# The second expert table's rows of two token tiles, laid a token to a partition and summed on VectorE instead of TensorE

## Chip, cores and metric

One core of one Trainium2 chip. The metric is the device time of one execution in microseconds; the median of three runs counts. PE is TensorE, DVE VectorE, ACT ScalarE, POOL GpSimd and SP SyncE.

## What is computed

One layer of a decoder trunk for a prompt of 1024 tokens (8 tiles of 128) and 32 sample tokens (a ninth, short tile, number 8 or NT). After the mixers each token chooses 128 experts of 16384 (8 heads, 16 each), and a layer called PEER sums them:

```python
def expert_block(args):
    xk, ik, gk = args                     # 128 tokens, their 8 x 16 experts, their weights
    act = gelu(einsum('nd,nhkd->nhk', xk, peer_u[ik]))
    coef = gk * act
    return einsum('nhk,nhkd->nd', coef, peer_v[ik])
...
x = layer_norm(ALPHA * x + g2 * y, ln2_g, ln2_b)
```

`peer_u` and `peer_v` are tables of 16384 rows of 1024 floats (4 KB a row). All is in float32.

## The kernel before

Four tiles (3 to 6, `DENSE`) go through **all** experts as dense products: 128 key rows of 128 experts. For each key row PE multiplies the split x of the four tiles with a block of `peer_u` (`psd`, 24 products of 512 columns, line 1067), ACT and DVE make the coefficients (`act` and `coef`, lines 1157 to 1165), and PE multiplies those with the block of `peer_v` (`po`, line 1174); DVE adds each `po` to the tile's sum (line 1183). Blocks of both tables are split into two halves of 16 bits by ACT and DVE (`us`, `vs`). Four key rows make a **group**: 96 `po` products, and 72 `psd` products of the next group, since every fourth key row has its `psd` made earlier, in a stage before (it is loaded back as `act`). There are 32 groups, 0 to 31. This is called the dense stage here.

The other five tiles (`GATHERED` = 0, 1, 2, 7, NT) fetch the rows that their tokens chose. For `peer_u` (`u_items`), step k fetches the k-th expert of each of 128 tokens, a token to a partition, by an indirect DMA on POOL's queue (512 KB), and DVE multiplies the tile with the tokens' x and adds along the row (line 1297; called U in the prediction). For `peer_v` (`v_items`), a step fetches the 128 experts of **one** token, an expert to a partition; PE multiplies them with a 128x32 matrix `cexp` that holds that token's 128 coefficients in one column (line 1354), so that the sum over partitions falls on that token's row of the PSUM tiles `acc0` and `acc1`. Two steps are issued together as four products (eight instructions in the trace). `cexp` comes from DVE (line 1344), and the coefficients and indices are transposed on PE for it at the end of `u_items`.

Gathered tiles run one behind another; the u steps of the next tile run beside the v steps of the one before. v rows of tiles 2, 7 and NT land in a ring of `NROW2` = 6 buffers of their own (`rows2`), u rows and the v rows of tiles 0 and 1 in one of 6 (`rows`). Tiles 2 and 7's and NT's v steps, and tile 7's and NT's u steps, lie in the dense stage.

The order is set by `run`: each part (here `g_main`, which runs the dense stage, and `g_gather`) yields costs for PE, DVE and DMA in us, and the part that is earliest on that account goes on; the framework's scheduler then orders the instructions by priority and its own timeline. `g_finish` (line 1411) multiplies a tile's sum with g2, adds x, and makes the LayerNorm.

Of the kernel before, what the change touches and what calls it, by code (L numbers as in the profile page):

```python
# [7 lines left out]
F32 = mybir.dt.float32  # L8
# [6 lines left out]
ALU = mybir.AluOpType  # L15
AX = mybir.AxisListType

P = 128
D = 1024
KD = D // P  # L20
NT = 8
# [22 lines left out]
    ("dense", {"g_gather": 0.8}),  # L44
)
NROW = 6
NROW2 = 6
AMPLE = 96
MB = 2.78
GATHERED = (0, 1, 2, 7, NT)  # L50
DENSE = (3, 4, 5, 6)
# [27 lines left out]
def kernel(ctx: ExitStack, tc: tile.TileContext, A, O):  # L79
    nc = tc.nc  # L80
    mm, tr = nc.tensor.matmul, nc.tensor.transpose
    V, S = nc.vector, nc.scalar
# [1191 lines left out]
    def u_items(t):  # L1274

        smp = t == NT
        n = NS if smp else P
        IF, G = (top[t][2][:, e].rearrange("p h j -> p (h j)") for e in range(2))
        x2 = cur["rows"].tile("x2u", [P, D])
        ii = keep("ii", [P, P], I32, bufs=2)  # L1280
        sv = keep("sv", [P, P], bufs=2)
        if smp:
            fr = keep("fr", [P, NS])
            for q in range(4):
                nc.sync.dma_start(x2[32 * q:32 * q + 32, :], x2_d[t, :NS, :])
                nc.sync.dma_start(fr[32 * q:32 * q + 32, :], IF[:NS, 32 * q:32 * q + 32])
            V.tensor_copy(ii[:, :NS], fr)
        else:
            nc.sync.dma_start(x2, x2_d[t])

        def step(k):
            if not smp and k % 16 == 0:
                V.tensor_copy(ii[:, k:k + 16], IF[:, k:k + 16])  # L1293
            s = gather("peer_u", ii[:, k:k + 1])

            def use():
                V.scalar_tensor_tensor(out=s, in0=s, scalar=1.0, in1=x2, op0=ALU.mult, op1=ALU.mult,  # L1297
                                       accum_out=sv[:, k:k + 1])
            return use

        for k in range(NS if smp else P):
            yield lambda k=k: step(k)

        def finish():
            if smp:
                s2 = keep("cT_", [P, P], bufs=2)[:NS]
                for q in range(4):
                    nc.sync.dma_start(s2[:, 32 * q:32 * q + 32], sv[32 * q:32 * q + 32, :NS])
                a = s2
            else:  # L1310
                a = sv
            S.activation(a[:n], a[:n], AF.Gelu)
            V.tensor_mul(a[:n], a[:n], G[:n])
            pt = psum.tile([P, 2, P], F32, name="ptc", tag="g", bufs=1)
            tr(pt[:, 0, :n], a[:n], ident[:n, :n])
            tr(pt[:, 1, :n], IF[:n], ident[:n, :n])
            cT_ = keep("cT_", [P, P], bufs=2)
            iT = keep("iT", [P, P], I32, bufs=2)
            V.tensor_copy(cT_[:, :n], pt[:, 0, :n])
            V.tensor_copy(iT[:, :n], pt[:, 1, :n])  # L1320
            coef[t] = (cT_, iT)
        yield finish

    def v_items(t):


        smp = t == NT
        cT_, iT = coef[t]
        pv = [psum.tile([P, 512], F32, name=f"acc{e}", tag=f"acc{e}", bufs=1) for e in range(2)]
        nj = 8 if smp else 32  # L1330
        hold = {}
        for j in range(nj):
            for q in range(4):

                def step(j=j, q=q):
                    if j % 2 == 0 and q == 0:
                        ce_ = hold["c"] = cur["rows"].tile("cexp", [P, 2, 4, 32], F32, 2)
                        if smp:
                            cv = cT_[:, 4 * j:4 * j + 8].rearrange("p (j q) -> p j q", q=4)
                            dv = delta[:, :, 32 - 4 * j:64 - 4 * j].rearrange("p (j q) c -> p j q c", q=4)  # L1340
                        else:
                            cv = cT_.rearrange("p (q j) -> p j q", q=4)[:, j:j + 2, :]
                            dv = delta[:, 0:2, 32 - j:64 - j].unsqueeze(2).to_broadcast([P, 2, 4, 32])
                        V.tensor_tensor(out=ce_, in0=cv.unsqueeze(3).to_broadcast([P, 2, 4, 32]), in1=dv, op=ALU.mult)
                    tok = 4 * j + q if smp else 32 * q + j
                    hold[q % 2] = gather("peer_v", iT[:, tok:tok + 1], t not in GATHERED[:2]), hold["c"][:, j % 2, q, :]
                    if q % 2 == 0:
                        return lambda: None
                    rows = hold[0], hold[1]

                    def add(b, e):
                        g = 32 * (q - 1 + b ^ 2 * e)
                        s, l = rows[b]
                        return mm(pv[e][g:g + 32, :], lhsT=l, rhs=s[:, e * 512:e * 512 + 512], start=(j == 0),  # L1354
                                  stop=(j == nj - 1), skip_group_check=True)

                    def use():
                        first = add(1, 0)
                        with tc.issue_after(first.ins):
                            add(1, 1)  # L1360
                            add(0, 0)
                            add(0, 1)
                    return use
                yield step

        def finish():
            src = pv
            if smp:
                src = []
                f = cur["rows"].tile("row", (P, D), F32, NROW)  # L1370
                fs = [f[:, 0:512], f[:, 512:1024]]
                for e in range(2):
                    (S.activation(fs[e], pv[e], AF.Copy) if e else V.tensor_copy(fs[e], pv[e]))
                yield 0, 1.2, 0
                for e in range(2):
                    b = bank("pfold")
                    mm(b[:NS], lhsT=fold, rhs=fs[e], start=True, stop=True)
                    src.append(b)
                yield 1.8, 0, 0
            if R:  # L1380
                yield from g_finish(t, NS if smp else P, src)
            else:
                finish_tile(t, NS if smp else P, src)
        yield finish
# [25 lines left out]

    def g_finish(t, n, src):
        x, g2 = ahead.pop(t)
        z = cur["rows"].tile("row", (P, D), F32, NROW)
        if t == NT:
            for e in range(2):
                c = slice(e * 512, e * 512 + 512)
                V.tensor_mul(z[:n, c], src[e][:n], g2[:n, c])
        else:
            sums_to(z, src)
            V.tensor_mul(z, z, g2)  # L1420
        yield 0, 1.2, 0
        V.tensor_add(z[:n], z[:n], x[:n])
        yield 0, 1.2, 0
        ln_rows(z, n, (R["ln2_g"], R["ln2_b"]))
        yield 0, 4.2, 0
        nc.sync.dma_start(O["y_s"] if t == NT else O["y_p"][t * P:(t + 1) * P, :], z[:n])
        yield 0, 1.2, 1.5
# [136 lines left out]
    def g_gather():  # L1564
# [6 lines left out]
        while todo or us or vs or done:  # L1571
# [20 lines left out]
            elif vs:  # L1592
# [13 lines left out]
                iv += 1  # L1606
                if done[0] == GATHERED[1] and iv == AMPLE:
                    ready.add("ample")
                c = 0.43, 0, 1.46
            else:  # L1610
                yield from wait(need or (todo[0], 0))
                continue
# [113 lines left out]
```

## Time and profile before

| | |
|---|---|
| median of 3 runs | 3274.7 us (3269.59 to 3281.56) |
| the profiled execution | 3260.78 us, its span 3259.1 us |
| busy share of the span | PE 84%, DVE 68%, POOL 41%, ACT 29% |
| mean granted clock of PE | 0.904 of 2.4 GHz |
| moved by DMA | 964.85 MB, mean 296 GB/s |

Busy time of an engine is the time in which at least one of its instructions ran. "Idle before, releaser" is the time an engine sat idle ahead of an instruction, and what ended it. The dense stage takes the span from about 1895 us to the end.

### The profile page before, as it was taken

The numbers are of one execution on the slowest core, as the hardware profiler recorded it, in microseconds if no ns is written. First come the engines' busy times: TensorE is split into PE (matmuls) and PEld (weight loads), VectorE is DVE, ScalarE is ACT, GpSimd is POOL, SyncE is SP. The second block draws the span as 40 slices with busy tenths as digits, with TensorE's granted clock in tenths as the row PEclk, the third lists the DMA queues.
The fourth block names the chain that finished last, engine by engine and source line by source line (L and its number), as shares of the span: only waits on it lengthen the run. The fifth ranks groups of instructions, "written<-read, shape, count | busy, mean of one in ns | idle before, by whom it ended". The sixth has DMA issues, their size and how long they took to land.

```text
span 3259.1 us, 44856 instructions
## 1 busy us (share of the span) xinstructions
PE 2740.2 (84%) x16366; PEld 1409.0 (43%) x16366; DVE 2206.8 (68%) x5763; ACT 938.7 (29%) x1618; POOL 1346.1 (41%) x1096
## 2 busy tenths in 40 slices
PE   6888984487976867998764699999999999999996
PEld 2447942344654425664333333343333433334443
DVE  2443998876788557988878547677677754456557
ACT  3323243111111013333446522222222222223331
POOL 0000366535445454544764527556554534440000
PEclk8888997698977878999886799999999999999998
DMA  8654798899998988888899989999999989994442
GB/s 295 232 180 145 281 350 306 291 321 322 334 328 298 328 315 294 290 289 321 285 326 348 351 298 359 360 363 381 372 378 340 384 300 326 352 321 136 141 129 75
DMA packets 370576, 964.85 MB, mean 296 GB/s; under 512 B 36933, under 2 KB 114884, under 8 KB 366252
## 3 DMA queue, kind: packets, MB, share of 16 engines
q0 software_dynamic: 156672, 570.49, 48.2%
q1 hardware_dynamic: 213684, 391.51, 34.7%
q8 instruction: 128, 2.10, 0.3%
q14 instruction: 92, 0.75, 0.1%
HBM read 892.92 MB, written 69.02 MB: 295 GB/s over the span
## 4 chain that ended last, share of the span: by engine, by line
PE 50%; DMA 14%; DVE 10%; issue 4%; POOL 2%; ACT 2%; SPq 0%; POOLq 0%; DVEq 0%; ACTq 0%
PE po L1174 18%; PE psd L1067 15%; PE acc L1354 6%; DMA row<-in_peer_v,iT 5%; DMA row<-in_peer_u,ii 5%; PE pqr L881 3%; DVE row L1297 3%; PE py L809 2%; POOL row L1270 2%; DMA v<-in_peer_v 1%; PE pvp L280 1%; PE pgm L1054 1%; DMA g<-G_d 1%; ACT gs L1057 1%; PE ps L886 0%
## 5 line engine op out<-in xcount | busy, mean ns | idle before, releaser
L1270 POOL DMA_INDIRECT row<-in_peer_u,ii x544 | 688.4, 1265 | 821.0 <-DVE ii L1293 316.9
L1270 POOL DMA_INDIRECT row<-in_peer_v,iT x544 | 655.4, 1205 | 717.7 <-PE acc L1354 460.5
L1297 DVE SCALAR_TENSOR_TENSOR row<-row,x2u 128x1024 f32<-128x1024 f32 x544 | 657.8, 1215 | 175.8 <-DMA row<-in_peer_u,ii 149.5
L1067 PE MATMUL psd<-xd,us 128*128 128x512 f16 x3072 | 722.6, 387 | 27.6 <-ACT us L1084 24.2
L1174 PE MATMUL po<-vs,coef 128*128 128x512 f16 x3072 | 700.8, 380 | 35.8 <-ACT coef L1164 20.3
L1174 PEld LDWEIGHTS <-coef 128*128 128x128 f16 x3072 | 294.0, 98 | 458.5 <-issue 89.5
L1067 PEld LDWEIGHTS <-us 128*128 128x128 f16 x3072 | 297.1, 100 | 450.8 <-issue 84.4
L1354 PE MATMUL acc<-row,cexp 128*32 128x512 f32 x2176 | 334.2, 665 | 139.5 <-DMA row<-in_peer_v,iT 128.2
L881 PE MATMUL pqr<-x2T,wpq 128*128 128x128 f32 (+1 forms) x2304 | 285.8, 285 | 8.3 <-ACT scores L892 7.0
L881 PEld LDWEIGHTS pqr<-x2T,wpq 128*128 128x128 f32 x2304 | 278.5, 201 | 21.9 <-ACT scores L892 7.2
L1159 DVE SCALAR_TENSOR_TENSOR act<-act,scale,g 128x512 f32<-128x512 f32 x128 | 96.1, 751 | 281.2 <-ACT act L1157 268.1
L1157 ACT ACTIVATE act<-psd,scale 128x512 f32<-128x512 f32 x96 | 65.9, 687 | 640.6 <-PE psd L1067 640.5
L1183 DVE SCALAR_TENSOR_TENSOR acc<-po,scale,acc 128x512 f32<-128x512 f32 x248 | 184.1, 746 | 84.0 <-PE po L1174 83.5
L1138 DVE SCALAR_TENSOR_TENSOR vs<-v,vs 128x1024 f16<-128x1024 f32 x128 | 155.9, 1219 | 62.3 <-ACT vs L1137 62.3
L1137 ACT ACTIVATE vs<-v 128x1024 f16<-128x1024 f32 x128 | 133.5, 1051 | 150.4 <-PE po L1174 90.1
L1054 PE MATMUL pgm<-ab 128*128 128x128 f16 x1024 | 97.3, 250 | 80.6 <-DVE ab L1044 42.8
L1354 PEld LDWEIGHTS acc<-row,cexp 128*32 128x32 f32 x2176 | 47.7, 112 | 266.1 <-DMA row<-in_peer_v,iT 166.6
L809 PE MATMUL py<-wo,Y 128*128 128x512 f32 (+1 forms) x288 | 138.9, 631 | 15.5 <-DMA Y<-ycat_d 14.3
L1057 ACT ACTIVATE gs<-pgm 128x256 f32<-128x256 f32 x256 | 124.6, 639 | 58.7 <-PE pgm L1054 45.9
L280 PEld LDWEIGHTS <-w 128*128 128x128 f16 x2160 | 123.0, 100 | 24.0 <-issue 20.8
L1121 DVE SCALAR_TENSOR_TENSOR us<-u,us 128x1024 f16<-128x1024 f32 x96 | 117.3, 1223 | 22.7 <-ACT us L1120 22.7
L1054 PEld LDWEIGHTS <-ab 128*128 128x128 f16 x1024 | 79.2, 113 | 117.9 <-issue 55.2
(343 smaller groups left out, 2857.1 us busy)
## 6 DMA issues: line engine op xcount, KB each, us to landing
v<-in_peer_v SPq DMA_DIRECT2D x128, 512.0 KB
u<-in_peer_uT SPq DMA_DIRECT2D x96, 512.0 KB
wpq<-in_w_pq SPq DMA_DIRECT2D x64, 512.0 KB
G_d<-gs SPq DMA_DIRECT2D x32, 1024.0 KB
g<-G_d SPq DMA_DIRECT2D x32, 1024.0 KB
wada<-in_w_ada SPq DMA_DIRECT2D x48, 512.0 KB
wf<-in_w_in SPq DMA_DIRECT2D x44, 512.0 KB
wo<-in_w_o SPq DMA_DIRECT2D x32, 512.0 KB
```

What stands on the lines that cost most here:

```text
L280: mm(out, lhsT=x if cs is None else y, rhs=y if cs is None else x, start=(i + k == 0), stop=(i == len(ps) - 1 and k == KD - 1))
L809: mm(py[t, e][:ns[t]], lhsT=Y_[t][:, k + j, :ns[t]], rhs=w[:, j, :], start=(k + j == 0), stop=(k + j == KD - 1))
L881: mm(pq[:, i * P:i * P + ns[t]], lhsT=w[:, k, :], rhs=X2[t][:, k, :ns[t]], start=(k == 0), stop=(k == KD - 1))
L1054: mm(pg[:, j, :], lhsT=ab[:, 0, t4 + j, :], rhs=ab[:, 1 + e, t4 + j, :], start=(e == 0), stop=(e == 1))
L1057: S.activation(gs[e][:, :, t0:t0 + 4].rearrange("p c t -> p t c"), pg[:, :, 64 * e:64 * e + 64], AF.Copy)
L1067: mm(ps, lhsT=us[a][:, k, :], rhs=xd[:, :, b, k, :], start=(m == 0), stop=(m == 23))
L1138: V.scalar_tensor_tensor(out=vs[:, 1], in0=v, scalar=SV, in1=vs[:, 0], op0=ALU.mult, op1=ALU.subtract)
L1174: mm(po, lhsT=d[:, a, i * P:(i + 1) * P], rhs=vs[:, b, c % 2, :], start=(m == 0), stop=(m == 3 * GROUP - 1))
L1183: V.scalar_tensor_tensor(out=a, in0=po, scalar=scale[:, 3:4], in1=a, op0=ALU.mult, op1=ALU.add)
L1270: nc.gpsimd.indirect_dma_start(out=s[:], out_offset=None, in_=A[table], in_offset=bass.IndirectOffsetOnAxis(ap=idx, axis=0))
L1297: V.scalar_tensor_tensor(out=s, in0=s, scalar=1.0, in1=x2, op0=ALU.mult, op1=ALU.mult, accum_out=sv[:, k:k + 1])
L1354: return mm(pv[e][g:g + 32, :], lhsT=l, rhs=s[:, e * 512:e * 512 + 512], start=(j == 0), stop=(j == nj - 1), skip_group_check=True)
```

## The change

For tiles 2 and 7 (`BY_TOKEN`), `u_items` ends without the transposes. A v step then fetches the k-th expert of each of 128 tokens, as the u steps do, and DVE multiplies it with that token's k-th coefficient (a column of `sv`) and adds it to a tile `vsum` in SBUF. After 128 steps `g_finish` goes on from `vsum`. The `rows2` ring shrinks by one buffer; a v step of these tiles is booked as 1.22 us of DVE instead of 0.43 us of PE. Tiles 0, 1 and NT stay as they were.

```diff
-NROW2 = 6
+NROW2 = 5
 AMPLE = 96
+BY_TOKEN = (2, 7)
...
             V.tensor_mul(a[:n], a[:n], G[:n])
+            if t in BY_TOKEN:
+                coef[t] = (sv, ii)
+                return
             pt = psum.tile([P, 2, P], F32, name="ptc", tag="g", bufs=1)
...
+    def v_items_by_token(t, cf, ix):
+
+        z = cur["rows2"].tile("vsum", (P, D))
+
+        def step(k):
+            s = gather("peer_v", ix[:, k:k + 1], True)
+
+            def use():
+                if k == 0:
+                    V.tensor_scalar(z, s, cf[:, 0:1], None, op0=ALU.mult)
+                else:
+                    V.scalar_tensor_tensor(out=z, in0=s, scalar=cf[:, k:k + 1], in1=z, op0=ALU.mult, op1=ALU.add)
+            return use
+
+        for k in range(P):
+            yield lambda k=k: step(k)
+
+        def finish():
+            yield from g_finish(t, P, z)
+        yield finish
+
     def v_items(t):
...
         cT_, iT = coef[t]
+        if t in BY_TOKEN:
+            yield from v_items_by_token(t, cT_, iT)
+            return
...
     def g_finish(t, n, src):
         x, g2 = ahead.pop(t)
-        z = cur["rows"].tile("row", (P, D), F32, NROW)
-        if t == NT:
+        z = src if t in BY_TOKEN else cur["rows"].tile("row", (P, D), F32, NROW)
+        if t in BY_TOKEN:
+            V.tensor_mul(z, z, g2)
+        elif t == NT:
...
-                c = 0.43, 0, 1.46
+                c = (0, 1.22, 1.46) if done[0] in BY_TOKEN else (0.43, 0, 1.46)
```

The order of instructions at three places. First DVE in the middle of the dense stage, from the `act` of one key row on. Before, with a `cexp` product now and then (`act`, `coef`, `us`, `vs` and `acc` are the dense stage's; `row,sv` is U):

```order
L1159 SCALAR_TENSOR_TENSOR act<-act,scale,g_18832 128x512
L1121 SCALAR_TENSOR_TENSOR us<-u,us 128x1024
L1138 SCALAR_TENSOR_TENSOR vs<-v,vs 128x1024
L1297 SCALAR_TENSOR_TENSOR row,sv<-row,x2u 128x1024
L1165 TENSOR_TENSOR coef<-act,coef 128x512
L1297 SCALAR_TENSOR_TENSOR row,sv<-row,x2u 128x1024 x2
L1159 SCALAR_TENSOR_TENSOR act<-act,scale,g_18832 128x512
```

and with the change, at a like place:

```order
L1160 SCALAR_TENSOR_TENSOR act<-act,scale,g_18088 128x512
L1122 SCALAR_TENSOR_TENSOR us<-u,us 128x1024
L1298 SCALAR_TENSOR_TENSOR row,sv<-row,x2u 128x1024
L1339 SCALAR_TENSOR_TENSOR vsum<-row,sv,vsum 128x1024
L1298 SCALAR_TENSOR_TENSOR row,sv<-row,x2u 128x1024
L1166 TENSOR_TENSOR coef<-act,coef 128x512
L1139 SCALAR_TENSOR_TENSOR vs<-v,vs 128x1024
L1298 SCALAR_TENSOR_TENSOR row,sv<-row,x2u 128x1024
L1160 SCALAR_TENSOR_TENSOR act<-act,scale,g_18088 128x512
L1339 SCALAR_TENSOR_TENSOR vsum<-row,sv,vsum 128x1024
```

The sums (`vsum`) now stand between the operations that make the coefficients for PE. Second, the same engine where tile 7's sum ends:

```order
L787 SCALAR_TENSOR_TENSOR vsum<-vsum,mv,r_ln_b 128x1024
L1423 SCALAR_TENSOR_TENSOR x1f<-x1f,r_ln_g 32x1024
L1424 SCALAR_TENSOR_TENSOR x1f<-r_ln_b,x1f 32x1024
L1372 TENSOR_TENSOR cexp<-cT__22846,delta 128x256 x2
L1401 COPY row<-acc_23586 128x512
L1447 TENSOR_TENSOR row<-pfold,g2s 32x512 x2
```

The last `cexp` of the sample tile and the copy of its sum stand behind tile 7's LayerNorm (line 787). Third, the end of POOL's queue, before:

```order
L1270 DMA row<-in_peer_u,ii 128x1024 x3
L1270 DMA row<-in_peer_v,iT 128x1024 x2
L1270 DMA row<-in_peer_u,ii 128x1024 x3
L1270 DMA row<-in_peer_v,iT 128x1024 x3
L1270 DMA row<-in_peer_u,ii 128x1024
L1270 DMA row<-in_peer_v,iT 128x1024
L1270 DMA row<-in_peer_u,ii 128x1024 x2
L1270 DMA row<-in_peer_v,iT 128x1024 x128
```

and with the change:

```order
L1271 DMA row<-in_peer_v,ii 128x1024 x16
L1271 DMA row<-in_peer_u,ii 128x1024 x6
L1271 DMA row<-in_peer_v,ii 128x1024
L1271 DMA row<-in_peer_u,ii 128x1024 x26
L1271 DMA row<-in_peer_v,ii 128x1024 x123
L1271 DMA row<-in_peer_v,iT 128x1024 x32
```

Before, the last 128 gathers are the end of tile 7's (96) and the sample tile's 32. With the change nearly all of tile 7's v rows come behind the last u row, and the sample tile's 32 behind those; on PE the sample tile's 64 products stand in one piece, five groups ahead of the end.

## Rows read from the trace of the kernel before

**Rows 1.** The page: busy time of each engine (us, share of the span, instructions), and the shares of the chain of work that ended last, by engine.

```profile
PE 2740.2 (84%) x16366; PEld 1409.0 (43%) x16366; DVE 2206.8 (68%) x5763; ACT 938.7 (29%) x1618; POOL 1346.1 (41%) x1096
...
PE 50%; DMA 14%; DVE 10%; issue 4%; POOL 2%; ACT 2%; SPq 0%; POOLq 0%; DVEq 0%; ACTq 0%
```

**Rows 2.** Windows of 100 us: length, then busy us (instructions) of PE, PE's weight loads, DVE, ACT and POOL, PE's granted clock, DMA share, GB/s.

```profile
400.00:500.00 100.00, 87.53 (x655) 50.41 (x652) 95.36 (x312) 46.02 (x67) 63.13 (x46) 0.96 0.98 347
500.00:600.00 100.00, 43.44 (x250) 29.04 (x250) 89.91 (x230) 26.10 (x45) 69.13 (x54) 0.66 0.86 301
...
800.00:900.00 100.00, 95.67 (x574) 60.64 (x574) 69.16 (x233) 11.28 (x31) 49.53 (x44) 0.88 0.92 334
900.00:1000.00 100.00, 81.26 (x545) 55.87 (x546) 80.83 (x346) 17.14 (x38) 45.97 (x41) 0.81 0.94 339
...
2300.00:2400.00 100.00, 92.71 (x458) 37.12 (x457) 73.72 (x105) 27.68 (x35) 58.35 (x50) 0.98 1.00 377
...
2500.00:2600.00 100.00, 100.00 (x497) 40.71 (x496) 78.52 (x125) 29.21 (x38) 60.11 (x50) 1.00 1.02 385
...
2700.00:2800.00 100.00, 99.64 (x530) 35.39 (x528) 42.71 (x54) 26.21 (x33) 46.98 (x46) 1.00 0.96 341
...
3000.00:3100.00 100.00, 100.00 (x465) 45.35 (x464) 51.19 (x62) 32.82 (x42) 0.00 (x0) 1.00 0.40 129
```

**Rows 3.** The chain in order of time: start us, length us, what. The first po product, one group without gathers, and the last.

```profile
1894.64 3.88 PE po L1174 x18
...
2938.39 5.18 PE psd L1067 x24
...
2953.93 10.36 PE po L1174 x48
...
2974.65 5.18 PE psd L1067 x24
...
3207.75 14.04 PE po L1174 x65
```

**Rows 4.** Groups of instructions by line from 1900 to 2920 us: busy us, mean ns of one, idle before and releasers. The products of gathered rows.

```profile
L1354 PE MATMUL acc<-row,cexp 128*32 128x512 f32 x1224 | 165.1, 604 | 0.4 <-DMA row<-in_peer_v,iT 0.4
```

**Rows 5.** DVE in order of time, in the dense stage: start us, length us. Two U with their accumulator reads.

```profile
2419.55 1.22 DVE L1297 SCALAR_TENSOR_TENSOR row<-row,x2u 128x1024 f32<-128x1024 f32 x1
2420.69 0.08 DVE L1297 DVE_READ_ACCUMULATOR row<-row,x2u 128x1 f32 x1
2420.69 1.22 DVE L1297 SCALAR_TENSOR_TENSOR row<-row,x2u 128x1024 f32<-128x1024 f32 x1
2421.84 0.08 DVE L1297 DVE_READ_ACCUMULATOR row<-row,x2u 128x1 f32 x1
```

**Rows 6.** DVE in order of time, in the tail: an operation on two SBUF tiles with a scale from a tile, and the one behind it.

```profile
3244.69 1.28 DVE L786 SCALAR_TENSOR_TENSOR acc<-acc,mv,r_ln_b 128x1024 f32<-128x1024 f32 x1
3245.89 0.15 DVE L361 TENSOR_TENSOR mv<-vy,vy 128x1 f32<-128x1 f32 x1
```

**Rows 7.** DVE in order of time, in the dense stage: a small operation (line 358) and one that reads its result (line 359).

```profile
2874.46 0.14 DVE L358 TENSOR_TENSOR vy<-vy 128x1 f32<-128x1 f32 x1
2874.63 0.16 DVE L359 TENSOR_TENSOR vy<-vy,ve 128x1 f32<-128x1 f32 x1
```

**Rows 8.** POOL in order of time while only v rows were gathered: start us, length us of an issue, and in brackets the idle time before it and what ended it.

```profile
2794.39 0.94 POOL L1270 DMA_INDIRECT row<-in_peer_v,iT  x1 [0.30 <-DMA row<-in_peer_v,iT]
2795.63 0.94 POOL L1270 DMA_INDIRECT row<-in_peer_v,iT  x1 [0.30 <-issue]
2798.73 1.06 POOL L1270 DMA_INDIRECT row<-in_peer_v,iT  x1 [2.16 <-PE acc L1354]
```

**Rows 9.** A window of 50 us in that stretch, POOL's gather issues alone: busy us (count), granted clock, DMA share, GB/s.

```profile
2750.00:2800.00 50.00, 24.21 (x23) 1.00 0.95 339
```

**Rows 10.** DMA from 2000 to 2650 us: the total, and issues by line with count, KB of one and, for gathers, median us to landing.

```profile
DMA packets 100247, 237.04 MB, mean 365 GB/s; under 512 B 7347, under 2 KB 38067, under 8 KB 100208
...
v<-in_peer_v SPq DMA_DIRECT2D x58, 512.0 KB
u<-in_peer_uT SPq DMA_DIRECT2D x45, 512.0 KB
g<-G_d SPq DMA_DIRECT2D x15, 1024.0 KB
act<-sd_d SPq DMA_DIRECT2D x15, 256.0 KB
```

**Rows 11.** DMA from 2670 to 2920 us: the v rows' gathers, count and median us from issue to landing.

```profile
row<-in_peer_v,iT POOLq DMA_INDIRECT x112, 7.5
```

**Rows 12.** POOL's gather issues from 2000 to 2600 us: ns of one, shortest/median/longest, first and last start.

```profile
L1270 POOL DMA_INDIRECT row<-in_peer_u,ii x146: 935/941/1992, 2004.5 to 2593.3; - x146
L1270 POOL DMA_INDIRECT row<-in_peer_v,iT x145: 935/1089/2779, 1999.8 to 2599.9; - x145
```

**Rows 13.** The same from 400 to 600 us.

```profile
L1270 POOL DMA_INDIRECT row<-in_peer_u,ii x100: 935/1110/4157, 399.9 to 599.1; - x100
```

**Rows 14.** Waits from 1900 to 2920 us: who waited for whom, total us, times, longest us.

```profile
DVE act L1159 <- ACT act L1157: 170.4, 50, 7.4
...
DVE vs L1138 <- ACT vs L1137: 50.8, 29, 14.7
...
DVE row L1297 <- DMA row<-in_peer_u,ii: 10.9, 6, 4.0
```

## The prediction

> **What bounds the kernel now.** I read the page's totals first: PE is busy for 84% of the span, DVE for 68%, and half of the chain that ended last is PE's [rows 1]. An average over unlike stages decides nothing, so I cut the span into windows. From 1900 us, the dense stage, PE is busy 93 to 100% at a granted clock of 0.98 to 1.00, which is its upper level of 2.4 GHz, while DVE stands at 43 to 79% [rows 2]. The chain, followed in order of time, shows the same: from the first po product at 1894.64 to the end of the last at 3207.75 + 14.04 = 3221.8 it is nearly all PE [rows 3]. So this stage, 1327.2 us, is PE's, and the change takes work from PE there and gives it to DVE. Where nothing is gathered, a group of four key rows repeats every 2974.65 - 2938.39 = 36.26 us: 168 products of 10.36/48 = 0.216 us [rows 3]. In that stretch DVE is busy 51.2% [rows 2], so 18.6 us of a group. A pair of gathered rows costs PE 8 instructions; 1224 of them took 165.1 us, so 1.08 us a pair [rows 4].
>
> To test the method I add up PE's own work in the kernel before, from the first po to the last: 1146 us of psd and po and 157 pairs, 1315 us. Measured are 1327, so 12 us were lost to waits.
>
> **The change, part by part.** Up to just ahead of the dense stage the five engines' instructions stand in the same order as before: 1894.6 us stay. What follows is in PE's groups, with counts from the changed program's order.
>
> *Taken from PE:* 128 pairs of tiles 2 and 7, 128 x 1.08 = 138 us. This is the most the change can give. The cexp products that go (32 on DVE, 0.4 us each) stood beside other work. ACT loses the copies of two sums, and the two transposes ahead of each by-token sum go too; none of that is on the path.
>
> *Put on DVE:* 256 operations of 128x1024. The trace of before has none with this chain (a running sum that each reads and writes, scaled by a column of a tile). The lower bound is U, the product with x2: it starts every 2420.69 - 2419.55 = 1.14 us [rows 5]. L786 is nearer, two tiles in SBUF and a scale read from a tile: 1.28 us, 1.20 us from start to start [rows 6]. Two chained operations back to back wait for the first one's end: 0.14 us became 0.17 from start to start where independent ones overlap [rows 7]; that gives 1.31, for the 29 or so that stand next to each other. I take 1.22 us, between 1.14 and 1.31: 312 us, 292 to 335.
>
> *Groups 0 to 2* keep 13 pairs of tile 1: 3 x 36.26 + 13 x 1.08 = 123 us, PE's.
>
> *Groups 3 to 17* (DVE's part of them by the order): 15 x 18.6 = 278, 157 U at 1.145 = 180, 102 of the new sums at 1.22 = 124, and 16 of LayerNorm for finished tiles: 599 us. PE's part is 15 x 36.26 = 544. Here **DVE becomes the bound**, most of all in groups 9 to 13 with 21 or 22 rows each.
>
> *Groups 18 to 26:* PE 9 x 36.26 = 326 us. DVE 8 x 18.6 + 115 x 1.22 + some 28 = 317. PE sets it, with 3% to spare.
>
> *The sample tile.* Its 64 products now stand in one block on PE, behind nothing but the last sum of tile 7, and its 32 gathers stand behind all of tile 7's on POOL. Behind the block on PE wait pfold and the five last groups; on DVE, the copy of its sum and the po sums behind that. Before, these products lay between others and cost 16 x 1.08 = 17 us. Now rows 6 to 32 each need one of five buffers back. POOL's bound is 0.94 + 0.30 us an issue [rows 8], 27 x 1.24 = 33 us; the rate of tile 7 before, 23 rows in 50 us [rows 9], is the other end, 27 x 2.17 = 59. DMA has little else to move during the block, so I take 45, nearer to POOL's bound.
>
> *The last five groups* after the block, 768 products: 166 us. The tail on DVE is unchanged, 3259.1 - 3221.8 = 37.3.
>
> Sum: 1894.6 + 123 + 599 + 326 + 45 + 166 + 37.3 = 3191 us, without losses.
>
> *Losses.* Of two engines that wait for each other in order, neither runs at 100%. The best filled window of DVE has it at 95.4%, the next at 89.9% [rows 2]. At 95.4% the 599 become 628 and the 317 become 332, 6 over PE's 326: 35 us. The 12 us of before for late loads stay. 3191 + 35 + 12 = **3238 us** against the span of 3259.1, so -21. The profiled execution took 3260.8; the median of the runs shown is 3274.7, 0.4% more, so I forecast 3274.7 - 21 = 3254 us, -0.6%.
>
> *The gathers.* Their number and bytes don't change: 512 KB each. Before, 2000 to 2650 us ran at 365 GB/s on the mean [rows 10] and lost PE few us. Groups 9 to 13 ask for 22 x 0.524 + 5.0 = 16.5 MB in 44 us, 375 GB/s; the mean of 3 to 17 is 350. So DMA is no worse covered than before. The rows2 ring goes from 6 buffers to 5. A row takes 0.30 + 0.94 + 7.5 us from the freed buffer to landing [rows 8, 11]; in groups 18 to 26 a sum comes every 36.26/14.4 = 2.5 us, so five buffers allow 12.6 us. It holds on the mean, but not behind four sums in a row.
>
> *The port.* POOL's issue takes 0.94 us at its shortest, but up to 2.8 us in 2000 to 2600, with a median of 1.09 for the v rows [rows 12]; in 400 to 600, where DVE is busy 90 to 95%, the median is 1.11 [rows 13]. So a busy DVE lengthens some issues, not most. The Trainium skill, SBUF — State Buffer, section Who interferes with whom, says that a VectorE instruction with two inputs in SBUF contends with a GpSimd instruction that reads SBUF, and that the one which started first holds the pair until its end. By that rule the sums, all with two such inputs, would hold up issues wherever they meet; the trace agrees for some, by the 2.8 us, and not for the median. What it would cost if most were held is a rival below.
>
> **The rivals.**
> 1. *No losses (0.16).* The order has spread the sums so evenly that DVE stays filled over 98%, and the sample block runs at POOL's 33 us. For it: before, U waited for its rows only 10.9 us in 1020 [rows 14]. 3191 - 12 + 12 = 3191, -68: 3207 us.
> 2. *DVE waits in front of a sum (0.22; slower).* A sum whose row is late blocks every act, coef, us and po sum behind it in DVE's order, and with them PE, which before waited with nothing but its products. In the clumps of sums in groups 18 to 26 the sixth stands some 9 us behind the first's start, and needs its buffer: 1.2 us until the first ends and 8.7 for the round trip. Before, DVE already waited 170 us for ACT's act and 51 for vs, which cost nothing while PE was the bound [rows 14]. At 89.9% busy [rows 2], 599 becomes 666 and 317 becomes 353: 3191 + 67 + 27 + 12 = 3297, +38: 3313 us. It decides from DVE busy below 93.4% in groups 3 to 26.
> 3. *Gathers are held up at the port (0.05).* With 1.99 us an issue, the longest of a u row from 2000 to 2600 [rows 12], and 0.30 between, the 108 gathers of groups 9 to 13 take 247 us where DVE needs 219: +28 on the forecast's 3238, so +7: 3282 us, no change that can be told. It is the rule of the page above, worked out for this queue.
> 4. *PE's clock (0.07; slower).* PE now waits for DVE in groups 3 to 17. From 800 to 900 it was busy 95.7% and granted 0.88; from 900 to 1000, 81% and 0.81; in 2300 to 2400, 92.7% and 0.98 [rows 2]. At 0.88 groups 18 to 26 take 371 us, 39 more than the 332: 3277, +18: 3293 us.
>
> That the change doesn't do what it says is excluded: the order holds no product for rows of tiles 2 and 7, and 254 chained sums and two scalings instead.
>
> **How the numbers follow.** A measurement of this kernel can tell about 0.3% (10 us) from no change. The forecast, DVE filled 93.5 to 98%, has 0.50: 0.38 of it faster than 3265 us, 0.12 within. With rival 1, faster has 0.54; with rival 3, no change has 0.17; rivals 2 and 4 give slower 0.29. The range goes from 3200, rival 1 with a sum nearer 1.19 us, to 3325, rival 2 with the block at 59: less than 2 in 10 lie outside.
>
> **What would show it.** Right: the acc products on PE fall by 1024 instructions and some 138 us; DVE is busy over 93% from some 2020 to 2980 us while PE falls to 85 to 90% in the first two thirds; the new sum lasts 1.28 us; near 2990 us there is a stretch of some 30 us on PE, filled with acc products that wait for rows, and behind it groups of 36.26 us. Wrong: DVE waits for rows of more than 50 us in all, a group of 18 to 26 longer than 39 us, a granted clock below 0.95, or POOL's issues above 1.5 us on the median.

## The result, and the profile after

The changed kernel takes 3220.86 us (median of 4 runs, 3215.36 to 3227.35) against 3277.88 us: ratio 0.983, 95% interval 0.9801 to 0.9859. That is 1.7% faster where 0.6% was forecast. The profiled execution took 3215.36 us, its span 3213.7 us.

The page's totals, as [rows 1]: PE lost 107 us of busy time and DVE gained 276. The chain that ended last is no longer half PE's.

```profile
PE 2633.7 (82%) x15338; PEld 1407.6 (44%) x15338; DVE 2482.8 (77%) x5983; ACT 936.7 (29%) x1612; POOL 1420.5 (44%) x1096
...
PE 26%; DVE 18%; issue 14%; DMA 13%; POOL 7%; ACT 2%; POOLq 0%; SPq 0%; DVEq 0%; ACTq 0%
```

Windows of 100 us of the changed kernel, columns as in [rows 2] (PE, weight loads, DVE, ACT and POOL busy, PE's granted clock, DMA share, GB/s):

```profile
2000.00:2100.00 100.00, 96.95 (x449) 43.77 (x448) 100.00 (x142) 30.94 (x40) 58.20 (x42) 1.00 0.97 350
...
2300.00:2400.00 100.00, 89.37 (x384) 38.72 (x383) 99.88 (x130) 27.34 (x35) 67.15 (x48) 0.93 1.00 366
2400.00:2500.00 100.00, 88.23 (x376) 38.25 (x376) 98.51 (x125) 25.41 (x33) 54.37 (x42) 0.91 0.97 347
...
2700.00:2800.00 100.00, 99.80 (x464) 45.03 (x462) 96.71 (x102) 32.83 (x42) 53.72 (x38) 1.00 0.93 332
...
2900.00:3000.00 100.00, 61.46 (x275) 20.13 (x273) 62.66 (x79) 17.21 (x22) 46.01 (x40) 0.74 0.84 290
```

From 2000 to 2500 us DVE is full, at 98.5 to 100%, and PE, which falls from 97 to 88%, waits for it; from 2600 PE is full again; near 2950 both stand half idle. To measure the three stretches I take the first accumulation (line 1183, now 1184) of a group as its start. DVE in order of time, start and length, before, for groups 0, 3, 18 and 27:

```profile
1905.69 2.73 DVE L1181 TENSOR_SCALAR acc<-po,scale 128x512 f32<-128x512 f32 x4
...
2021.99 1.40 DVE L1183 SCALAR_TENSOR_TENSOR acc<-po,scale,acc 128x512 f32<-128x512 f32 x2
...
2677.77 0.75 DVE L1183 SCALAR_TENSOR_TENSOR acc<-po,scale,acc 128x512 f32<-128x512 f32 x1 [0.88 <-PE po L1174]
...
3071.38 0.75 DVE L1183 SCALAR_TENSOR_TENSOR acc<-po,scale,acc 128x512 f32<-128x512 f32 x1 [0.64 <-PE po L1174]
```

and after:

```profile
1905.22 2.71 DVE L1182 TENSOR_SCALAR acc<-po,scale 128x512 f32<-128x512 f32 x4
...
2025.20 1.40 DVE L1184 SCALAR_TENSOR_TENSOR acc<-po,scale,acc 128x512 f32<-128x512 f32 x2
...
2623.56 2.71 DVE L1184 SCALAR_TENSOR_TENSOR acc<-po,scale,acc 128x512 f32<-128x512 f32 x4
...
3025.57 0.72 DVE L1184 SCALAR_TENSOR_TENSOR acc<-po,scale,acc 128x512 f32<-128x512 f32 x1
```

| us | before | after | forecast |
|---|---|---|---|
| groups 0 to 2 | 116.3 | 120.0 | 123 |
| groups 3 to 17 | 655.8 | 598.4 | 599, with loss 628 |
| groups 18 to 26 and the block | 393.6 | 402.0 | 326 + 6 + 45 |
| from group 27 to the end of the span | 187.7 | 188.1 | unchanged |

So the gain lies in groups 3 to 17, 57 us there; the other stretches together lost 12, and the two profiled executions lie 45 us apart. (The medians lie 57 us apart: the profiled execution before was 17 us faster than its median, so the equal numbers are chance.) In groups 18 to 26, 42 pairs (45 us of PE) went away, and the stretch still became 8 us longer.

The place is the block of the sample tile. PE in order of time, the last dense products ahead of it, its first pairs, its last, and what follows:

```profile
2936.74 5.34 PE L1175 MATMUL po<-vs,coef 128*128 128x512 f16 x24
2955.21 1.93 PE L1382 MATMUL acc<-row,cexp 128*32 128x512 f32 x8 [13.13 <-DMA row<-in_peer_v,iT]
2962.65 1.93 PE L1382 MATMUL acc<-row,cexp 128*32 128x512 f32 x8 [5.51 <-DMA row<-in_peer_v,iT]
...
3015.99 1.94 PE L1382 MATMUL acc<-row,cexp 128*32 128x512 f32 x8 [1.35 <-DMA row<-in_peer_v,iT]
3018.75 3.62 PE L1405 MATMUL pfold<-row,fold 128*32 128x512 f32 x4 [0.82 <-DVE row L1401]
3022.30 5.35 PE L1175 MATMUL po<-vs,coef 128*128 128x512 f16 x24
```

and POOL, whose first gather for the sample tile waits for a sum of tile 7 to free a buffer, and the fourth for PE:

```profile
2943.77 1.86 POOL L1271 DMA_INDIRECT row<-in_peer_v,iT  x1 [0.66 <-DVE vsum L1339]
...
2957.41 0.94 POOL L1271 DMA_INDIRECT row<-in_peer_v,iT  x1 [8.69 <-PE acc L1382]
```

Each pair waits for its rows (the number in brackets). The block has three parts: 13.1 us to the first pair, 60.8 us for the 15 steps of a pair after it (3015.99 - 2955.21, 4.05 each), and 6.3 from the start of the last pair to the next po: 80 us on PE, and 74 by the accumulations, since DVE was still 6 us behind PE when the block began.

### The profile page after: what moved, and what is told of

Its sections match the earlier page's. It is cut to its first block, busy times and chain, and to the rows that moved or that the text cites. A ratio compares the mean times of both kernels' runs of the same rounds, so it can differ in the third digit from the quotient of the medians.

```text
span 3213.7 us, 43217 instructions
## 1 busy us (share of the span) xinstructions
PE 2633.7 (82%) x15338; PEld 1407.6 (44%) x15338; DVE 2482.8 (77%) x5983; ACT 936.7 (29%) x1612; POOL 1420.5 (44%) x1096
## 4 chain that ended last, share of the span: by engine, by line
PE 26%; DVE 18%; issue 14%; DMA 13%; POOL 7%; ACT 2%; POOLq 0%; SPq 0%; DVEq 0%; ACTq 0%
POOL row L1271 7%; PE psd L1068 7%; PE po L1175 6%; DMA row<-in_peer_v,iT 5%; DVE row L1298 5%; DMA row<-in_peer_u,ii 4%; PE pqr L882 3%; PE acc L1382 3%; PE py L810 2%; DVE vsum L1339 2%; DMA G_d<-gs 1%; DVE acc L1184 1%; DVE vs L1139 1%; PE pgm L1055 1%; PE pvp L281 1%
## 5 line engine op out<-in xcount | busy, mean ns | idle before, releaser
L1271 POOL DMA_INDIRECT row<-in_peer_u,ii x544 | 712.1, 1309 | 840.4 <-DVE ii L1294 314.9
L1068 PE MATMUL psd<-xd,us 128*128 128x512 f16 x3072 | 715.0, 387 | 33.3 <-ACT us L1085 24.2
L1271 POOL DMA_INDIRECT row<-in_peer_v,iT x288 | 351.9, 1222 | 403.7 <-PE acc L1382 193.8
L1175 PEld LDWEIGHTS <-coef 128*128 128x128 f16 x3072 | 302.8, 99 | 440.2 <-issue 67.6
L1271 POOL DMA_INDIRECT row<-in_peer_v,ii x256 | 354.3, 1384 | 313.1 <-DVE vsum L1339 254.8
L1382 PE MATMUL acc<-row,cexp 128*32 128x512 f32 x1152 | 208.0, 766 | 181.2 <-DMA row<-in_peer_v,iT 179.7
L1339 DVE SCALAR_TENSOR_TENSOR vsum<-row,sv,vsum 128x1024 f32<-128x1024 f32 x254 | 324.6, 1278 | 3.4 <-DMA row<-in_peer_v,ii 2.0
L1055 PE MATMUL pgm<-ab 128*128 128x128 f16 x1024 | 99.3, 253 | 78.5 <-DVE ab L1045 40.5
L1165 ACT ACTIVATE coef<-act 128x512 f16<-128x512 f32 x128 | 80.4, 628 | 275.4 <-DVE act L1160 258.9
L1382 PEld LDWEIGHTS acc<-row,cexp 128*32 128x32 f32 x1152 | 27.7, 119 | 272.5 <-DMA row<-in_peer_v,iT 219.3
```

The source lines that it names most:

```text
L1055: mm(pg[:, j, :], lhsT=ab[:, 0, t4 + j, :], rhs=ab[:, 1 + e, t4 + j, :], start=(e == 0), stop=(e == 1))
L1068: mm(ps, lhsT=us[a][:, k, :], rhs=xd[:, :, b, k, :], start=(m == 0), stop=(m == 23))
L1175: mm(po, lhsT=d[:, a, i * P:(i + 1) * P], rhs=vs[:, b, c % 2, :], start=(m == 0), stop=(m == 3 * GROUP - 1))
L1271: nc.gpsimd.indirect_dma_start(out=s[:], out_offset=None, in_=A[table], in_offset=bass.IndirectOffsetOnAxis(ap=idx, axis=0))
L1339: V.scalar_tensor_tensor(out=z, in0=s, scalar=cf[:, k:k + 1], in1=z, op0=ALU.mult, op1=ALU.add)
```

## The experiments

Medians, ratios against the kernel before on the same chip, and the **dense span** of the profiled execution, from the first accumulation to the last. (Where the first one falls differs by some 20 us from run to run, 1901 to 1922 us, with nearly the same order ahead of it; the dense span leaves that out. Each dense span is that of one execution, and the executions of one kernel lie up to 26 us apart, so a difference of some 10 us in it decides nothing by itself.)

| kernel | median us | ratio (95%) | dense span |
|---|---|---|---|
| before | 3277.88 | 1 | 1329.1 |
| the change | 3220.86 | 0.983 (0.9801 to 0.9859) | 1284.1 |
| e1 only tile 2 | 3240.12 | 0.9917 (0.989 to 0.9943) | 1297.0 |
| e2 only tile 7 | 3266.39 | 0.9991 (0.9971 to 1.0011) | 1328.0 |
| e3 NT ahead of 7 | 3187.92 | 0.9765 (0.973 to 0.9801) | 1252.7 |
| e4 two rings | 3209.94 | 0.9825 (0.9794 to 0.9857) | 1269.9 |
| e5 half sums | 3217.48 | 0.9853 (0.9807 to 0.9898) | 1279.6 |
| e6 = e2 with NT ahead of 7 | 3231.22 | 0.987 (0.9837 to 0.9902) | 1296.0 |
| e7 = e3 with e4 | 3163.44 | 0.9667 (0.9627 to 0.9706) | 1226.3 |
| e8 old cost row | 3297.76 | 1.008 (1.0052 to 1.0108) | 1364.1 |
| e9 half rows, full sums | 3202.24 | 0.98 (0.9771 to 0.9829) | 1268.3 |
| e10 half rows, half sums | 3146.77 | 0.9626 (0.9593 to 0.9658) | 1219.8 |
| e11 = e7, later u steps | 3181.73 | 0.9729 (0.9695 to 0.9763) | 1240.0 |
| e12 before, NT ahead of 7 | 3290.49 | 1.0073 (1.0042 to 1.0104) | 1357.7 |

### Which tile pays: e1, e2, e6

```diff
-BY_TOKEN = (2, 7)
+BY_TOKEN = (2,)                  # e1
+BY_TOKEN = (7,)                  # e2 and e6
...
-GATHERED = (0, 1, 2, 7, NT)
+GATHERED = (0, 1, 2, NT, 7)      # e6 alone
```

> Only tile 2 is summed on DVE; tile 7 goes back to PE, in pairs that lie beside the sample tile's, so there is no block of sample products. Theory A (the forecast without its losses: DVE filled 98% and more where it is the bound, PE's pairs at 1.08 us elsewhere, and in the full change some 57 us lost in the sample tile's block beyond its own 17): DVE's part of groups 3 to 15 is 517 us, PE's of 16 to 31 649, with 123 for groups 0 to 2: 1289 us from the first po on, against 1277 by the same sum for the full change (block of 74 us in it). So some 12 us longer than the full change: 3233 us, 45 less than before. Rival B (the gain is tile 2's alone, since tile 7's is given back in the block and in groups 18 to 26): no longer than the full change, 3221 us or less. Rival C (the gain comes from the other edits, the ring of 5 and the cost table, and not from PE's pairs): 3221 as well.

Measured: the dense span is 12.9 us longer than the change's, as theory A had it. The ratios put it at 0.9 points, 28 us; that is wider, and their intervals leave room for 13. Tile 2 alone gives 32 of the change's 45 us of dense span. Rivals B and C, by which this kernel would be no slower than the change, fall.

> Only tile 7 is summed on DVE; tile 2's rows go to PE again. DVE's work never runs ahead of PE's in the order (by group 15: 447 us against 663), so PE is the bound throughout. Theory A: PE's own 1245 us and 57 us lost in the block, which is there in the order again: 1302 us, 25 more than the full change: 3246 us, 32 less than before. DVE busy some 60 to 80% in the first half of the dense stage. Rival B (tile 7's sums give nothing): 3278 us, as before. Rival C (ring and cost table): 3221 us.

Measured: nothing is gained, 0.9991. Theory A's sign for the block was right, its size not: in the order of e2 more of tile 7's sums stand ahead of the sample tile's rows, and PE's first pair comes after a wait of 38.13 us instead of 13.13:

```profile
2905.67 3.83 PE L1068 MATMUL psd<-xd,us 128*128 128x512 f16 x17
2947.63 1.93 PE L1382 MATMUL acc<-row,cexp 128*32 128x512 f32 x8 [38.13 <-DMA row<-in_peer_v,iT]
```

That wait is 25 us longer; the dense span came out 44 us over the change's, where theory A had 25. Rival B's time, that of the kernel before, is the one that came out here; e6 decides against its reason.

> Only tile 7 is summed on DVE, and the sample tile is gathered ahead of it, so there is no block. By the order PE's own work is 1245 us, and one clump of DVE's work (76 us in the group that closes the u steps of tile 7) costs some 20 more. Theory A (with only tile 7 on DVE everything gained, 69 us of PE, went into the block of the sample tile, 95 us in that run, and into groups 14 and 15): 1265 + 12 for late loads against the 1328 us measured with the block: 3266 - 51 = 3215 us. Rival G (the rows of tile 7 cost PE nothing before, since its last third ran where PE had time): within 10 us of 3266.

Measured: 3231 us, 1.2% less than e2. So tile 7's sums do pay when there is no block, and rivals B and G fall. The rest of what was expected went into a wait of the same kind at another place: `pfold`, the product behind the sample tile's sum, waits for DVE's copy of it (line 1401), which stands behind the clump of u steps.

```profile
2642.08 5.34 PE L1068 MATMUL psd<-xd,us 128*128 128x512 f16 x24
2692.99 3.62 PE L1405 MATMUL pfold<-row,fold 128*32 128x512 f32 x4 [45.57 <-DVE row L1401]
```

### The block: e3, e4, e7, e8, e11, e12

```diff
-GATHERED = (0, 1, 2, 7, NT)
+GATHERED = (0, 1, 2, NT, 7)      # e3, e7, e11; e12 in the kernel before
...
-hold[q % 2] = gather("peer_v", iT[:, tok:tok + 1], t not in GATHERED[:2]), ...
+hold[q % 2] = gather("peer_v", iT[:, tok:tok + 1], t not in GATHERED[:2] and not (smp and tok % 2)), ...   # e4, e7, e11
...
-c = (0, 1.22, 1.46) if done[0] in BY_TOKEN else (0.43, 0, 1.46)
+c = 0.43, 0, 1.46                # e8
...
-iu * nv <= 1.4 * (iv - ...
+iu * nv <= (0.5 if done[0] == NT else 1.4) * (iv - ...     # e11
```

> The sample tile is gathered ahead of tile 7 instead of behind it (the order of the gathered tiles is 0, 1, 2, NT, 7), all else as in the change. Its 64 products then lie in four pieces in groups 16 to 18 and not in one block. Theory A (the block costs some 57 us beyond its own 17): 123 for groups 0 to 2, DVE's 565 us for 3 to 16 and PE's 542 for 17 to 31: 1230 us against 1277, so 3221 - 47 = 3174 us; PE's granted clock stays above 0.95 from 2500 us to the end of the groups. Rival D (the products wait for their rows wherever they stand, and the DVE work that they push aside comes later): within 10 us of 3221.

Measured: 0.65 points less than the change; dense span -31.4 us, of 47 expected. No sample product waits for its row any more, and rival D falls. PE's clock was granted at 0.90 in the window of group 15 (53 us long, PE waiting for DVE's and ACT's `vs`), so the clause on the clock failed there.

> The kernel before (all rows summed on PE), with the sample tile ahead of tile 7 as in e3. Theory A (the block is made by the change; before, the sample products lay between others and cost their 17 us, so moving them gives nothing): PE's 1314 us stay, and a clump of 60 us of DVE's work in group 18, 16 over PE's, is new: 3269 + 10 = 3279 us. Rival L (the sample tile's place costs in either kernel): 3237 us, as much less as e3 was under the change.

Measured: 0.7% slower than before; `pfold` waits there for DVE's copy:

```profile
2682.38 3.27 PE L1377 MATMUL pfold<-row,fold 128*32 128x512 f32 x4 [26.78 <-DVE row L1373]
```

The same edit that takes 31 us of dense span from the changed kernel adds 29 to the kernel before: the block is made by the change. Rival L falls.

> Every second row of the sample tile lands in the ring of the u rows (6 buffers, which is idle by then) and not in rows2 (5 buffers): up to 11 rows of it under way. Theory A (the block is set by the round trip of 5 buffers: 1.97 us a row, from 2955 to 3018 us): with 11 buffers POOL's 1.24 us or the DMA's 1.4 us a row (512 KB at 365 GB/s) is left, 32 rows in 40 to 45 us from the first issue on: the block falls from 80 to some 60 us, 3221 - 20 = 3201 us. Rival E (PE's halved clock and the work behind the sums set the block): within 7 us of 3221.

Measured: group 26 with its block 88.1 us instead of 110.6; the dense span -14.2. The first pair waited 12.29 us, about as in the change; the 15 steps behind it took some 40 us, 2.7 each instead of 4.05:

```profile
2968.70 1.94 PE L1382 MATMUL acc<-row,cexp 128*32 128x512 f32 x8 [12.29 <-DMA row<-in_peer_v,iT]
...
3007.41 3.42 PE L1382 MATMUL acc<-row,cexp 128*32 128x512 f32 x12 [1.46 <-DMA row<-in_peer_v,iT]
3011.62 1.90 PE L1405 MATMUL pfold<-row,fold 128*32 128x512 f32 x4 [0.78 <-DVE row L1401]
```

So the ring of 5 set the block's pace, and the first wait, which a second ring leaves, goes with the place behind tile 7's sums. The ratios (0.9825 and 0.983) can't tell the 14 us.

> The change without its new cost row: a v step of tiles 2 and 7 is booked as 0.43 us of PE again. The order moves only late: the sample tile's block on PE now stands at the end of group 23 instead of 26, while 55 of tile 7's sums instead of 11 stand on DVE behind the point that PE has reached by then. Theory A (PE's block waits for DVE to get through the sums ahead of the sample tile's rows, and nothing is given back behind it): DVE's part of groups 18 to 24 is 309 us, then the block's some 60, then 253 for the rest: 1335 against 1277, so 3216 + 58 = 3274 us. Rival C (the cost table is without effect on time): within 7 us of 3216.

Measured: slower than the kernel before. PE stood 100 us for the first sample row, while DVE went through 57 sums of tile 7. The cost row is thus worth 2.5% of the time by where it puts one block:

```profile
2810.95 2.75 PE L1175 MATMUL po<-vs,coef 128*128 128x512 f16 x12
2913.85 1.94 PE L1382 MATMUL acc<-row,cexp 128*32 128x512 f32 x8 [100.15 <-DMA row<-in_peer_v,iT]
```

> Both in one: the sample tile ahead of tile 7, and every second row of it in the ring of the u rows. Theory A: with the sample tile ahead of 7, 143 us of PE's idle time in front of sample and other products were left in waits for rows, 31 us more than by its sum in groups 15, 16, 18 and 19; with two rings the rows are there earlier, and the order spreads DVE's work better (groups 10 to 16 at 36 to 39 us of DVE instead of 40 to 46). The larger of DVE and PE, group by group, sums to 1194 us against 1210 with one ring: 3188 - 16 - 15 (half of the waits) = 3157 us. Rival H (the u rows of tile 7 now wait for buffers that the sample rows hold, and DVE with them): 3188 us or more.

Measured: 3163 us, ratio 0.9667: 1.7% less than the change, near what was expected. One reason that I gave was wrong: the 143 us of idle time were the whole span's, and e3 has no such wait in the dense stage. What came with the gain is the order's spread of DVE's work: groups 10 to 17 took 293 us with 121 gathers, where e3 took 344 with 154. No run separates this from the second ring itself. A short block is back in group 19 (78.5 us), where the last sample rows stand on POOL's queue among u rows of tile 7, and PE stands in front of each:

```profile
2644.97 1.06 PE L1382 MATMUL acc<-row,cexp 128*32 128x512 f32 x8
2669.34 1.93 PE L1382 MATMUL acc<-row,cexp 128*32 128x512 f32 x8 [11.75 <-DMA row<-in_peer_v,iT]
2685.82 3.79 PE L1382 MATMUL acc<-row,cexp 128*32 128x512 f32 x16 [14.54 <-DMA row<-in_peer_v,iT]
```

> As e7 (sample tile ahead of tile 7, its rows in two rings), and tile 7's u steps go at 0.5 of the pace of the sample tile's v steps instead of 1.4, so that 13 of them no longer stand ahead of the sample tile's last rows. In e7 group 19 lasted 78 us, 42 more than PE's own, with 27 us of PE waiting for sample rows. Theory A (PE waits for its sample rows as long as DVE's work that stands ahead of them lasts): half of the 42 goes, the clump of DVE's work now being 60 us in group 16 without sample products behind it: 3163 - 20 = 3143 us. Rival K (u steps that come later make a clump that costs as much): 3163 us.

Measured: 0.6 points slower than e7, worse than either theory. Later u steps only mixed them one by one between the last sample rows, and five pairs in a row waited:

```profile
2520.40 1.93 PE L1382 MATMUL acc<-row,cexp 128*32 128x512 f32 x8 [6.49 <-DMA row<-in_peer_v,iT]
2534.43 1.93 PE L1382 MATMUL acc<-row,cexp 128*32 128x512 f32 x8 [12.09 <-DMA row<-in_peer_v,iT]
2542.74 1.93 PE L1382 MATMUL acc<-row,cexp 128*32 128x512 f32 x8 [6.39 <-DMA row<-in_peer_v,iT]
```

### What bounds groups 3 to 17: e5, e9, e10

```diff
-V.scalar_tensor_tensor(out=z, in0=s, scalar=cf[:, k:k + 1], in1=z, ...)
+V.scalar_tensor_tensor(out=z[:, :512], in0=s[:, :512], scalar=cf[:, k:k + 1], in1=z[:, :512], ...)   # e5, e10
...
+src = A[table].rearrange("a (h d) -> (a h) d", h=2) if half else A[table]                            # e9, e10
...
+s2 = s[:, 0:512].unsqueeze(1).to_broadcast([P, 2, 512])   # e9: the half row, read twice
```

> Each sum of the change but the first takes 512 of the row's 1024 columns (the other half of the two tiles' sums is left out): about 0.60 us of DVE a step instead of 1.20, all gathers as in the change. The scheduler's order shifts with it: DVE takes more rows a group and the sample tile's products lie in three pieces instead of one block. Theory A (DVE sets groups 3 to 17 with its own work and next to no loss, and the block costs 57 us beyond its 17): DVE's part of 3 to 17 falls from 598 to some 555 us, PE's 544 just below it; no block: 123 + 555 + 510 = 1188 against 1277, so 3216 - 89 = 3127 us (against the full change at 0.983 of before). Rival F (DVE waits for rows, whose rate by DMA and POOL sets groups 3 to 17): the rows come no faster, groups 3 to 17 stay at 598 and more, and only the block goes: 3159 us.

Measured: 3217 us; the full change stands at 0.983 of before, this at 0.9853. Half of DVE's price of the sums is gone, and nothing was gained: neither theory's time came out, 3127 or 3159. Groups 18 to 26, which have no block now, took 53 us less than in the change, and groups 3 to 17 took 53 us more. Below is one window over groups 6 to 16 of each kernel, columns as in [rows 2]. First the change, 40.7 us a group:

```profile
2136.00:2584.00 448.00, 412.61 (x1829) 181.85 (x1827) 442.80 (x592) 130.03 (x166) 275.61 (x199) 0.96 0.99 360
```

and e5, 45.7 us a group:

```profile
2147.00:2650.00 503.00, 434.93 (x1844) 187.66 (x1843) 434.40 (x643) 128.81 (x166) 292.90 (x230) 0.92 0.97 351
```

In the change DVE is busy 98.8% and the DMA share is 0.99. In e5 neither DVE (86%) nor PE (86%) is full; the DMA share is 0.97, and the order has put 230 gathers into these eleven groups instead of 199. A share near 1 doesn't show a bound by itself: before, windows with 1.00 and 1.02 had PE busy 93 to 100% [rows 2]. The waits in e5's window say what PE lacked. It was `vs`, for which ACT waited for the loads of `v`:

```profile
PE po L1175 <- ACT vs L1138: 50.5, 16, 7.9
...
ACT vs L1138 <- DMA v<-in_peer_v: 37.9, 12, 12.4
```

In the change the same two waits are 5.2 and 6.6 us, from 2136 to 2584.

> As e5 (each sum takes 512 columns), and the v gathers of tiles 2 and 7 fetch only that half row as well (256 KB instead of 512 KB). The other half of the two tiles' sums is left out. Theory I (in e5, where 22 to 24 rows fall in a group, the DMA's rate took the place of DVE: groups 6 to 16 lasted 46 us on the mean with DVE busy 78 to 88% and the DMA 0.93 to 1.02): with half the bytes both limits are gone, PE's 36.3 us a group is left nearly everywhere: 1190 us against 1277, 3216 - 87 = 3129 us. Theory J (in e5 it was waits between DVE, ACT and PE, or POOL's issues, and not the bytes): 3217 us, as e5.

Measured: 3147 us, 2.3% less than e5. Groups 6 to 16 take 36.7 us, PE's own pace, and PE no longer waits for ACT's `vs`:

```profile
2148.00:2552.00 404.00, 391.72 (x1795) 175.90 (x1793) 386.97 (x577) 126.11 (x161) 234.39 (x182) 0.99 0.92 326
```

Rival J, by which this kernel would take as long as e5, falls. One caveat: the order has 182 gathers here, not 230; but over the whole dense span, with nearly the same number of gathers in both (454 and 455), e10 is 60 us shorter than e5.

> The v gathers of tiles 2 and 7 fetch half rows (2 KB a row, 256 KB a gather); each sum takes that half twice, so it still works on 1024 columns (the second half of the two tiles' sums is thus not the right one). DVE's work stays, 65 MB of gathers go. Theory A (DVE alone sets groups 3 to 17): by the order's counts the larger of DVE and PE, group by group, sums to 1214 us against 1211, and 20 sums instead of 11 stand behind the block on DVE: 3216 + 10 = 3226 us, no gain. Theory I (DMA, at 0.97 to 1.02 of its time in 2000 to 2500 us of the change, is the bound beside DVE; e5 stayed at 3217 us although each sum cost half): groups 8 to 14 fall by some 22 x 0.26 MB / 365 MB per ms = 4 to 8 us each where they are DMA's, at least 20 in all: 3195 us or less.

Measured: 0.98, dense span -15.8 us, between the two theories. With fewer bytes and full sums DVE stays at 98.8% of groups 6 to 16, 38.6 us each with 181 gathers:

```profile
2158.00:2583.00 425.00, 407.56 (x1848) 182.10 (x1848) 419.99 (x542) 133.07 (x166) 238.22 (x181) 0.98 0.87 301
```

So DVE sets these groups with fewer bytes too, and the 16 us can't be put down to the bytes alone: the order has moved rows as well. Groups 3 to 17 compare best, since no block lies in them: 598.4 us with 254 gathers in the change, 651.7 with 298 in e5, 582.5 with 239 in e9, 554.7 with 257 in e10. With about the change's rows, taking off both DVE's work and bytes gives 44 us, nearly down to PE's 544; taking off DVE's work alone, the loads came late. So DVE is the bound of the change there, and the DMA is close behind it. How much of e5's 53 us is its 44 more gathers isn't taken apart.

## Why the prediction was right in its mechanism and wrong in size

The mechanism came out as forecast: PE's pairs leave, DVE becomes the bound from group 3 on, PE again from 18 on, and a block of sample products gives part of it back. Two terms were mis-sized, with opposite signs, and the ends of the sum rest on a wrong reading.

- **The step that failed: *Losses*, +35 and +12.** I took DVE's filling, 95.4%, from the fullest window of an earlier stage [rows 2], and forecast 628 us for groups 3 to 17. Measured are 598.4 us, the 599 us of the sum without losses, at 98.5 to 100% in the windows to 2500 us. Rival 1 was right on this step, and wrong on the block. That two engines which wait for each other leave each other gaps did not show here: DVE's waits for ACT's `act`, 170.4 us before [rows 14], are 15.9 us after, and those for rows stay small. Waits from 1900 to 3000 us of the changed kernel:

```profile
PEld acc L1382 <- DMA row<-in_peer_v,iT: 51.5, 10, 13.6
PE acc L1382 <- DMA row<-in_peer_v,iT: 37.0, 11, 13.1
...
PE po L1175 <- DVE vs L1139: 22.5, 9, 4.5
DVE act L1160 <- ACT act L1158: 15.9, 12, 4.5
...
DVE vsum L1339 <- DMA row<-in_peer_v,ii: 2.0, 5, 0.9
```

  When DVE became the late engine, its operands mostly lay ready when it came to them; that ACT and PE had run ahead is argued from these waits, and no run takes it apart.
- **The 12 us for late loads, and the ends.** [rows 3] shows the longest pieces of the chain, and I took two of them for PE's first and last `po`. On PE the first starts at 1881.91, not 1894.64, and the last ends at 3207.59 + 26.06 = 3233.65, not 3221.8:

```profile
1881.91 1.89 PE L1174 MATMUL po<-vs,coef 128*128 128x512 f16 x4 [15.73 <-ACT coef L1164]
...
3207.59 26.06 PE L1174 MATMUL po<-vs,coef 128*128 128x512 f16 x120
```

  So PE's stretch before is 1351.7 us, and it lost 37 us over its own 1315, not 12; the start stands 13 us too late in the sum, and the tail, 25.4 us on PE, 12 too long.
- **The sample tile's block: 45 us priced, 74 measured** (402.0 less nine groups of 36.4, the mean of groups 18 to 25). My ends, 33 and 59, were both paces of rows 6 to 32. I left out the wait ahead of the first pair (13.1 us; e4 shows that it doesn't come from the ring), and the copy and `pfold` behind the last. The pace was near the slow end: 60.8 us for 30 rows, 2.03 a row, where my ends were 1.24 and 2.17.
- **Rechecked on PE**, from the first `po` of each group in the change: 1878.8 us ahead of it, 124.8 for groups 0 to 2, 602.3 for 3 to 17, 416.4 for 18 to 26 with the block, 165.9 for the last five and a tail of 25.4, together the span. The sum had 1894.6, 123, 599, 371, 166 and 37.3. So the sum without losses, 3191, missed the span by only 23 us in part by luck: 28 us too much at its two ends hid more than half of the 45 that were missing in groups 18 to 26.
- **The sum's price held.** It lasts 1.28 us, as I had said; with 1.22 us from start to start, groups 3 to 17 come out to 1 us (102 sums and 156 U lie there, 102 and 157 were counted).

```profile
L1339 DVE SCALAR_TENSOR_TENSOR vsum<-row,sv,vsum 128x1024 f32<-128x1024 f32 x254 | 324.6, 1278 | 3.4 <-DMA row<-in_peer_v,ii 2.0
```

- **Rival 2** (DVE waits ahead of a sum) fell for the change: 2.0 us in all. But e8, e2 and e6 show its mirror image, PE held by work that stands ahead of it on DVE, at 38 to 100 us a time.
- **Rival 3** (gathers held at the port) fell as a bound, though the issues did become longer: medians of 941 and 1089 ns before [rows 12] are 1429 and 1433 ns now, from 2000 to 2600 us:

```profile
L1271 POOL DMA_INDIRECT row<-in_peer_u,ii x158: 932/1429/7297, 1999.2 to 2596.9; - x158
L1271 POOL DMA_INDIRECT row<-in_peer_v,ii x105: 932/1433/3614, 2001.9 to 2531.2; - x105
```

  The Trainium skill, SBUF — State Buffer, section Who interferes with whom, has a VectorE instruction with two SBUF inputs contend with GpSimd reads; the trace agrees as far as the median goes, but POOL still had slack, at 54 to 67% busy, and rows were not late. That every two-input operation would hold an issue up, as I worked the rule out in the rival, is more than the medians show.
- **Rival 4** (PE's clock) showed in the windows, 0.93 and 0.91 from 2300 to 2500 us, with DVE busy 98.5 to 99.9%, so that it can have cost little. It stood under my 0.95, and groups 24 and 25, at 40.9 and 39.9 us, over my 39: two of my signs of being wrong, but neither marks the step that failed. In groups 18 to 25 the clock was near 1.00. In the block it was granted 0.50 (below).
- **DMA.** I called it "no worse covered than before". It was as full as before, 0.99 of its time in groups 6 to 16; what I didn't see is how close it stood behind DVE, so that e5 ran into late loads. The Trainium skill, HBM Reference, section Specifications (TRN2), gives about 425 GB/s for a core that streams alone; the full windows shown above, gathers of 4 KB rows beside plain loads, moved 347 to 366 GB/s, and that measured rate decides.

## What to carry to other kernels

When work moves from the engine that bounds a stage to another, don't carry over the losses that the second one shows where it was not the bound: here its own work was the time. Then look for the next limit: here the DMA lay close behind DVE, and half the price on DVE gained nothing alone. A piece of work that others used to hide becomes a block when it ends up alone on an engine's queue; price it from the wait ahead of its first item to the end of what follows it, not by its pace. Moving the block's source ahead in the order, alone or with a second ring (e3, e7), was worth 0.7 to 1.7% more, up to as much as the change itself.

## What the hardware showed that was not expected

PE's clock fell to 0.50 in the block (1.2 of 2.4 GHz), after a gap of 13 us ahead of the first pair and 0.6 to 5.5 us between pairs. Eight acc instructions then took 1.93 us, where the same eight took 1.06 in the dense stage (e7, at 2644.97). The po of the next group, at 3022.30, is at full speed from its start, 5.35 us for 24. Most of the halving was hidden in the waits for rows; `pfold` behind them took 3.62 us, where e4's took 1.90.

Busy time and granted clock from 2950 to 3000 us of the change:

```profile
2950.00:3000.00 50.00, 20.91 (x88) 2.25 (x88) 16.32 (x31) 0.00 (x0) 20.71 (x22) 0.50 0.86 294
```
